# Hybrid decoder block: the last normalisation split into half rows, with low halves begun one product earlier

## The chip, the cores and the metric

The kernel runs on one core of a Trainium2 chip. The metric is device time in microseconds, the median of several runs. A core has five engines with a queue of instructions each, which run side by side and wait for one another by semaphores: PE (TensorE, matrix products into PSUM banks), DVE (VectorE, elementwise), ACT (ScalarE, functions, copies and scalings of rows, with sums along a row on request), POOL (GpSimd, elementwise) and SP (SyncE, which issues DMA transfers). ACT issues some transfers too. An engine works through its queue in the order in which the program wrote it, so an instruction that waits holds up all that stand behind it.

## The reference

One layer on x of 1024 tokens by 1024 columns, in float32: a SwiGLU feed-forward half step, a mixing part with dilated attention and pooling, a second feed-forward half step, and a final row normalisation:

```python
h = h + 0.5 * swiglu(rms_norm(h, ffn1_norm[l]), ffn1_w1[l], ffn1_w3[l], ffn1_w2[l])
...
h = h + merged @ w_out[l]
h = h + 0.5 * swiglu(rms_norm(h, ffn2_norm[l]), ffn2_w1[l], ffn2_w3[l], ffn2_w2[l])
return rms_norm(h, final_norm)
```

with

```python
def rms_norm(x, g):
    y = xf * lax.rsqrt(jnp.mean(xf * xf, axis=-1, keepdims=True) + RMS_EPS)
    return (y * g.astype(jnp.float32)).astype(x.dtype)
```

The change concerns the last two lines: the second product of the second feed-forward step (its output g, 1024 by 2816, times w2, 2816 by 1024), its addition to h, and the final normalisation.

## The kernel before

The 1024 tokens lie in eight tiles of 128 rows, h[0] to h[7], each 128 by 1024. LOWS and HIGHS (line 283) are the slices of the first and the last 512 columns of a tile.

The down product g times w2 is computed as seven products of half-sized blocks instead of eight (the list DOWN, lines 97 to 105). Each product has a left operand (a sum of blocks of g that an earlier stage left in DRAM), a right operand (a block of w2, or the sum or difference of two), and a list of the quarters of the result to which it is added with a sign. A quarter is named (th, n): th = 0 means tiles 0 to 3 and th = 1 tiles 4 to 7, n = 0 the low and n = 1 the high columns. Tiles 0 to 3 are final after the fifth product (index 4, len(DOWN) - 3). The sixth (index 5) is added to the low and the high halves of tiles 4 to 7. The seventh (index 6) is added to the high halves of tiles 4 to 7 alone.

A product is cut into six steps along its inner dimension (PAIRS), five of two 128-deep slices and one of a single slice, so there are 42 steps, 0 to 41; the seventh product is steps 36 to 41. Every operand is held as two parts, high (rounded) and low (the remainder), and a matmul of two operands is three matmuls: high by high, low by high, high by low. A step of two slices is therefore 24 matmuls of 128x128 by 128x512 over the four row tiles, the last step 12.

Class Down writes the order out by hand (nothing is scheduled by a planner):

- `load(i)` (line 645) issues the transfer of step i's left operand on SP, three steps ahead.
- `begin(i)` (line 687) prepares step i, two steps ahead: `sums_w` (line 672) makes the sum of two weight blocks on DVE (tile s, line 684, one 128x512 operation a slice), then `split` (line 652) makes the parts of the right operand (bhi on ACT, line 664; blo, line 668) and of the left one (ahi on ACT, alo). The subtraction that makes a low part runs on DVE, or on POOL in every fourth call of `split`, which is the left operand of every odd step.
- `multiply(i, t)` (line 697) issues step i's matmuls for row tile t into bank t of its product (line 706).
- `add(m, t)` (line 708) adds bank t of product m to the tiles of h, one DVE operation of 128x512 for each quarter (line 711). A product's four adds are issued one a step, in the four steps behind the product's end, ahead of that step's `begin`. For the last product they follow its last two steps, whose matmuls are interleaved by row tile.
- `run` (line 713) is the loop over the steps. Its arguments `after`, called behind each add, and `tick` differ: FFN 1 passes a tick, FFN 2 none.

For FFN 2, `after2` (line 2012) does the final normalisation. For tiles 0 to 3 it is called behind the adds of product 4, for tiles 4 to 7 behind those of product 6. `norm_rows` (line 272) squares a whole row on ACT with its sum (line 259), takes the mean plus epsilon on DVE (line 263), raises it to the power -1/2 on POOL (line 264) and multiplies the row by the result and the gain in one DVE operation of 128x1024 (line 267); then SP stores it. Tile 7 alone is squared and scaled in two halves, low half squared ahead of the other, and its two halves are stored from SP and from ACT.

Buffers: `h_tile` gives one of eight 128x1024 buffers, all held by h[0] to h[7] at that time; the next ones it gives are those of h[0] to h[3] again, once they are read. `row` and `own_row` give other buffers of that size, `small` tiles of a few columns.

Of the kernel before, what the change touches and what calls it, by code (L numbers as in the profile page):

```python
# [10 lines left out]
F32 = mybir.dt.float32  # L11
F32R = mybir.dt.float32r
AF = mybir.ActivationFunctionType
OP = mybir.AluOpType
AX = mybir.AxisListType

P = 128
S = 1024
D = 1024
NT = S // P  # L20
# [3 lines left out]
EPS = 1e-6  # L24
HALF = 512
# [101 lines left out]
def tile_block(  # L127
# [28 lines left out]
    nc = tc.nc  # L156
# [7 lines left out]
    small = ctx.enter_context(sbuf("small", bufs=4))  # L164
# [9 lines left out]
    def row(name):  # L174
        return keep.tile([P, 1024], F32, tag="raw", bufs=RAW_BUFS, name=name)

    def h_tile(name):
        return keep.tile([P, D], F32, tag="h", bufs=NT, name=name)
# [93 lines left out]
    def norm_rows(t, gain, name, alloc=row):  # L272
        y = alloc(f"hn_{name}{t}")
        squares(t, y)
        inverse(t)
        scaled(t, y, gain)
        return y
# [347 lines left out]
    class Down:  # L625
# [26 lines left out]
        def split(self, side, srcs, n):  # L652
            hi, lo = (
                self.dp.tile([P, 2, HALF], F32R, tag=f"{side}{part}", bufs=3, name=f"{side}{part}_{self.name}{n}")
                for part in ("hi", "lo")
            )
            self.n_lo += 1
            whole = len(srcs) == 1 and srcs[0].shape[1] > 1
            eng = gp if self.n_lo % 4 == 0 else ve
            at = 0  # L660
            for src in srcs:
                n = src.shape[1]
                c = slice(at, at + n)
                ac.activation(hi[:, c], src, AF.Copy)  # L664
                for q in range(n if eng is gp else 1):
                    o = slice(q, q + 1) if eng is gp else slice(0, n)
                    d = slice(at + o.start, at + o.stop)
                    eng.tensor_tensor(lo[:, d], src[:, o], hi[:, d].bitcast(F32), op=OP.subtract)  # L668
                at += n
            return hi, lo  # L670
# [42 lines left out]
        def run(self, pool, after, tick=None):  # L713
            def half_tile(tag, n):
                return pool.tile([P, HALF], F32, tag=tag, bufs=4, name=f"{tag}_{self.name}{n}")

            self.half_tile = half_tile
            n = len(self.steps)
            done = []
            for i, (m, s) in enumerate(self.steps):  # L720
                if i < n - 2:
                    for t in range(4):
                        self.multiply(i, t)
                if i == n - 1:

                    for t in range(4):
                        self.multiply(i - 1, t)
                        self.multiply(i, t)
                        self.add(m, t)
                        after(m, t)  # L730
                if done:
                    self.add(*done[0])
                    after(*done.pop(0))
                if s == len(PAIRS) - 1:
                    done = [(m, t) for t in range(4)]
                self.ops.pop(i - 1, None)
                if m == len(DOWN) - 1 and tick is None:
                    raws.depth = max(3, len(PAIRS) + 1 - s)
                if i == 1:
                    next(self.parts, None)  # L740
                if i + 3 < n:
                    self.load(i + 3)
                if i + 2 < n:
                    self.begin(i + 2)
                if i == 0:
                    next(self.parts)
                if tick is not None:
                    tick(i)
# [1260 lines left out]
    def own_row(n):  # L2009
        return pool.tile([P, D], F32, tag="row", bufs=2, name=n)  # L2010

    def after2(m, t):
        if m != len(DOWN) - 3 and m != len(DOWN) - 1:
            return
        if m == len(DOWN) - 1:
            t += 4
        rows = slice(t * P, (t + 1) * P)
        if t < NT - 1:
            nc.sync.dma_start(out[rows, :], norm_rows(t, final_gain, "n4", own_row if t < 4 else row))
            return  # L2020
        y = row("hn_last")
        st = small.tile([P, 4], F32, tag="nlast", name="nst_last")
        for j in range(2):
            c = slice(j * HALF, (j + 1) * HALF)
            ac.activation(y[:, c], h[t][:, c], AF.Square, accum_out=st[:, j:j + 1])
        ve.tensor_scalar(st[:, 0:1], st[:, 0:1], 1.0 / D, EPS, op0=OP.mult, op1=OP.add)
        ve.scalar_tensor_tensor(st[:, 2:3], st[:, 1:2], 1.0 / D, st[:, 0:1], op0=OP.mult, op1=OP.add)
        gp.tensor_tensor(st[:, 3:4], st[:, 2:3], mhalf, op=OP.pow)
        for j in range(2):
            c = slice(j * HALF, (j + 1) * HALF)  # L2030
            ve.scalar_tensor_tensor(y[:, c], h[t][:, c], st[:, 3:4], final_gain[:, c],
                                    op0=OP.mult, op1=OP.mult)
            (nc.sync if j == 0 else nc.scalar).dma_start(out[rows, c], y[:, c])

    with sbuf("steps2", "right") as pool:
        raws.load()
# [94 lines left out]
```

## Time and profile before

| | us |
|---|---|
| runs of before: median of 3 | 1957.8 |
| lowest, highest | 1957.8, 1959.87 |
| profiled execution, first to last instruction | 1955.6 |
| its PE busy | 1914.1 |
| its DVE busy | 1343.5 |
| its ACT busy | 759.4 |
| its POOL busy | 741.1 |

The profile is of one execution, whose own time on the device is the span in the table; the runs are timed around the whole execution, so their median lies a little above. Rows of the timeline read: start and duration in us, engine, line of the kernel, operation, what it writes <- what it reads, shape, and how many like it were merged (x2 for two in a row). In brackets stands how long the engine sat idle before it, and which instruction ended that. An engine's name with a q (ACTq, SPq) is its queue issuing a transfer. Two DVE operations in a row overlap by some 0.08 us, so that a pair of 0.68 us each takes 1.28. Rows of groups read: line, engine, operation, shapes, xcount | busy us, mean ns | idle before it, by what ended it. Rows of windows give busy time and number of instructions of each engine in a stretch, then the granted PE clock, the share of the DMA engines in use and GB/s. Rows of transfers give the queue, how many, KB each, and the median us from issue to landing.

### The profile page before, as it was taken

What the parts mean: (1) busy time and instruction counts of PE and PEld (TensorE: products, weight loads), DVE (VectorE), ACT (ScalarE), POOL (GpSimd) and SP (SyncE); (2) the same over time, 40 slices, a digit from 0 to 9 for tenths busy, and PEclk for the clock granted to TensorE, in tenths of its full rate; (3) what the DMA queues carried; (4) which work ended last, traced back from release to release, by engine and by line L of the source; (5) the groups of instructions that cost most, each with busy time, mean ns of one, the idle gap of its engine ahead of it and who ended that gap; (6) DMA issues with size and microseconds to landing.
All of it is one profiled execution on the core that took longest, in us unless ns stands there. A gap on an engine that the chain in (4) does not pass through costs nothing. (4 is left out here: it accounts for less than half of the span.)

```text
span 1955.6 us, 25018 instructions
## 1 busy us (share of the span) xinstructions
PE 1914.1 (98%) x8938; PEld 1579.7 (81%) x8938; DVE 1343.5 (69%) x2012; ACT 759.4 (39%) x1361; POOL 741.1 (38%) x557
## 2 busy tenths in 40 slices
PE   9999999999999999999998999999999999999997
PEld 7788888888888887888876878887788888878885
DVE  7776556557686876568774886887665556577766
ACT  6333333334344533334344662253333333333343
POOL 5333333332222444445454365543333333322231
PEclk9999999999999999999998999999999999999999
DMA  4155223336465546765658887643523223454653
GB/s 185 44 194 169 85 86 117 121 124 208 156 246 201 167 120 230 232 220 185 232 218 289 241 241 261 253 161 96 190 102 135 82 87 120 139 204 135 212 195 142
DMA packets 147005, 333.57 MB, mean 171 GB/s; under 512 B 20160, under 2 KB 40896, under 8 KB 145344
## 3 DMA queue, kind: packets, MB, share of 16 engines
q1 hardware_dynamic: 138096, 308.00, 45.9%
q10 hardware_dynamic: 8784, 23.96, 3.5%
q8 instruction: 71, 1.16, 0.2%
q14 instruction: 54, 0.44, 0.1%
HBM read 229.61 MB, written 102.30 MB: 170 GB/s over the span
## 5 line engine op out<-in xcount | busy, mean ns | idle before, releaser
L706 PE MATMUL d_f<-bhi_f,alo_f 128*128 128x512 f32 x616 | 240.8, 391 | 2.4 <-POOL alo_f L668 2.2
L706 PE MATMUL d_f<-bhi_f,ahi_f 128*128 128x512 f32 x616 | 240.9, 391 | 0.2 <-ACT ahi_f L664 0.2
L706 PE MATMUL d_f<-blo_f,ahi_f 128*128 128x512 f32 x616 | 240.0, 390 | 0.0
L668 POOL TENSOR_TENSOR alo_f<-g_f,ahi_f 128x512 fp32r<-128x512 f32 x70 | 99.2, 1434 | 298.5 <-ACT ahi_f L664 289.8
L314 PE MATMUL u_mixm<-xhi_t_mix,wc_mixm 128*128 128x512 f32 x608 | 196.0, 393 | 2.7 <-POOL wc_mixm L306 2.3
L314 PE MATMUL u_mixm<-xhi_b_mix,wc_mixm 128*128 128x512 f32 x456 | 149.3, 393 | 2.0 <-DVE y_m L982 2.0
L706 PEld LDWEIGHTS d_f<-bhi_f,alo_f 128*128 128x128 f32 x616 | 115.7, 188 | 29.0 <-POOL alo_f L668 4.0
L314 PEld LDWEIGHTS u_mixm<-xhi_t_mix,wc_mixm 128*128 128x128 f32 x608 | 113.8, 188 | 29.0 <-POOL wc_mixm L306 4.9
L706 PEld LDWEIGHTS d_f<-bhi_f,ahi_f 128*128 128x128 f32 x616 | 115.8, 188 | 24.1 <-ACT ahi_f L664 0.6
L706 PEld LDWEIGHTS d_f<-blo_f,ahi_f 128*128 128x128 f32 x616 | 115.8, 188 | 23.8
L314 PE MATMUL u_mixm<-xlo_t_mix,wc_mixm 128*128 128x512 f32 x304 | 118.6, 390 | 0.0
L306 POOL TENSOR_TENSOR wc_mixm<-s_mixm,wc_mixm 128x512 fp32r<-128x512 f32 x52 | 75.8, 1459 | 99.7 <-ACT wc_mixm L303 84.0
L314 PEld LDWEIGHTS u_mixm<-xhi_b_mix,wc_mixm 128*128 128x128 f32 x456 | 85.7, 188 | 20.7 <-ACT late_hi L1125 2.8
L303 ACT ACTIVATE wc_mixm<-s_mixm 128x512 fp32r<-128x512 f32 x76 | 47.6, 629 | 122.8 <-DVE s_mixm L347 52.1
L314 PE MATMUL u_mixm<-xlo_b_mix,wc_mixm 128*128 128x512 f32 x228 | 88.9, 390 | 0.0
L664 ACT ACTIVATE ahi_f<-g_f 128x1024 fp32r<-128x1024 f32 x84 | 81.8, 974 | 2.0 <-DMA g_f<-gs_f 2.0
L306 POOL TENSOR_TENSOR wc_mixm<-raw,wc_mixm 128x512 fp32r<-128x512 f32 x40 | 60.4, 1515 | 44.9 <-ACT wc_mixm L303 42.0
L664 ACT ACTIVATE bhi_f<-s_f2w 128x512 fp32r<-128x512 f32 x55 | 32.8, 627 | 97.1 <-DVE s_f2w L684 86.8
L1854 PE MATMUL wo<-w_o,o_hi 128*128 128x512 f32 x224 | 69.3, 391 | 0.0
L314 PEld LDWEIGHTS u_mixm<-xlo_t_mix,wc_mixm 128*128 128x128 f32 x304 | 57.2, 188 | 11.7 <-DVE xlo_t_mix L385 0.2
L664 ACT ACTIVATE bhi_f<-s_f1w 128x512 fp32r<-128x512 f32 x55 | 32.9, 630 | 85.1 <-DVE s_f1w L684 80.2
L1616 PE MATMUL yp<-pool_in,wab 128*128 128x512 f32 x192 | 55.7, 426 | 4.2 <-DMA pool_in<-pool 4.2
(1300 smaller groups left out, 5099.8 us busy)
## 6 DMA issues: line engine op xcount, KB each, us to landing
g_f<-gs_f SPq DMA_DIRECT2D x70, 512.0 KB, 4.5
gs_f<-y_f SPq DMA_DIRECT2D x88, 256.0 KB, 2.3
raw<-in_w2a_dram SPq DMA_DIRECT2D x35, 512.0 KB, 4.1
raw<-in_w2b_dram SPq DMA_DIRECT2D x35, 512.0 KB, 4.0
gs_f<-gb_f SPq DMA_DIRECT2D x46, 256.0 KB, 2.3
raw<-in_w1a_dram SPq DMA_DIRECT2D x22, 512.0 KB, 4.6
raw<-in_w3a_dram SPq DMA_DIRECT2D x22, 512.0 KB, 6.3
raw<-in_w1b_dram SPq DMA_DIRECT2D x22, 512.0 KB, 4.5
```

The costliest lines, as they stand in the source:

```text
L303: ac.activation(w[:, 0], src, AF.Copy)
L306: eng.tensor_tensor(w[:, 1], src, w[:, 0].bitcast(F32), op=OP.subtract)
L314: pe.matmul(p, a, b, start=(start and k == 0 and q == 0), stop=(k == 3 and q == 2), skip_group_check=not start)
L664: ac.activation(hi[:, c], src, AF.Copy)
L668: eng.tensor_tensor(lo[:, d], src[:, o], hi[:, d].bitcast(F32), op=OP.subtract)
L706: pe.matmul(self.banks[m][t], l, r, start=(first and q == 0), stop=(last and q == 2))
L1616: pe.matmul(p, a, b, start=(j == 0), stop=(j == 11))
L1854: pe.matmul(banks[m][t], l, r, start=(st == 0 and j == 0 and q == 0), stop=(st == 1 and j == 1 and q == 2))
```

## The change

Three things are edited.

In `split`, a low part that would run on POOL runs on DVE in the last two steps; of those, only the left operand of step 41 is a fourth call. The test holds for both feed-forward steps.

In `run`, where there is no tick (FFN 2), `begin(41)` in step 39 is called ahead of the add of product 5 to tile 7 instead of behind it.

In the final normalisation, tiles 0 to 3 stay as they are. Tiles 4 to 7 are treated alike, in halves. `low_half` is called behind each add of product 5, in steps 36 to 39: it squares the low columns on ACT with their sum, adds epsilon on DVE, and multiplies the low columns by the gain on DVE into a buffer y. The rest follows the adds of product 6: `high_half` squares the high columns, `power` adds the two sums on DVE and raises to -1/2 on POOL, and `send_out` scales the high columns by the row's factor and the gain on DVE, stores them from SP, scales the low columns of y by the row's factor on ACT and stores them from ACT. `send_out` of a tile is called behind the next tile's add and `high_half`, ahead of that tile's `power`. The squares carry the factor 1/1024 inside (a scale of 1/32 ahead of the square).

The order of each engine's queue changes as follows, beside the moved operations. DVE: the add pair of each of tiles 4 to 7 is followed by one 128x1 and one 128x512 operation. ACT: a half square stands ahead of the roundings for step 38, 39 and 40, and a fourth one behind those of step 41; at the end the order is square 4, square 5, scaling and store of 4, square 6, scaling and store of 5, square 7, scaling and store of 6, scaling and store of 7. POOL: without the subtraction of step 41 in each FFN. SP: the same loads in the same order, then four stores of 256 KB instead of three of 512 KB and one of 256 KB. PE: unchanged.

```diff
@@ split @@
             whole = len(srcs) == 1 and srcs[0].shape[1] > 1
-            eng = gp if self.n_lo % 4 == 0 else ve
+            eng = gp if self.n_lo % 4 == 0 and n < len(self.steps) - 2 else ve
             at = 0
@@ run @@
                         self.add(m, t)
                         after(m, t)
+                ahead = i == n - 3 and tick is None
+                if ahead:
+                    self.begin(i + 2)
                 if done:
                     self.add(*done[0])
                     after(*done.pop(0))
...
-                if i + 2 < n:
+                if i + 2 < n and not ahead:
                     self.begin(i + 2)
@@ final normalisation @@
+    ends = {}
+
+    def low_half(t):
+
+        y, st = h_tile(f"n4_{t}"), small.tile([P, 4], F32, tag="nlast", name=f"nst_last{t}")
+        ac.activation(y[:, LOWS], h[t][:, LOWS], AF.Square, scale=D ** -0.5, accum_out=st[:, 0:1])
+        ve.tensor_scalar(st[:, 1:2], st[:, 0:1], EPS, None, op0=OP.add)
+        ve.tensor_tensor(y[:, LOWS], h[t][:, LOWS], final_gain[:, LOWS], op=OP.mult)
+        ends[t] = y, st
+
+    def high_half(t):
+        y, st = ends[t]
+        ac.activation(y[:, HIGHS], h[t][:, HIGHS], AF.Square, scale=D ** -0.5, accum_out=st[:, 2:3])
+
+    def power(t):
+        y, st = ends[t]
+        ve.tensor_tensor(st[:, 2:3], st[:, 2:3], st[:, 1:2], op=OP.add)
+        gp.tensor_tensor(st[:, 3:4], st[:, 2:3], mhalf, op=OP.pow)
+
+    def send_out(t):
+        y, st = ends.pop(t)
+        rows = slice(t * P, (t + 1) * P)
+        ve.scalar_tensor_tensor(y[:, HIGHS], h[t][:, HIGHS], st[:, 3:4], final_gain[:, HIGHS],
+                                op0=OP.mult, op1=OP.mult)
+        nc.sync.dma_start(out[rows, HIGHS], y[:, HIGHS])
+        ac.activation(y[:, LOWS], y[:, LOWS], AF.Copy, scale=st[:, 3:4])
+        nc.scalar.dma_start(out[rows, LOWS], y[:, LOWS])
+
     def after2(m, t):
-        if m != len(DOWN) - 3 and m != len(DOWN) - 1:
-            return
-        if m == len(DOWN) - 1:
-            t += 4
...
+        if m == len(DOWN) - 3:
+            rows = slice(t * P, (t + 1) * P)
+            nc.sync.dma_start(out[rows, :], norm_rows(t, final_gain, "n4", own_row))
+        elif m == len(DOWN) - 2:
+            low_half(4 + t)
+        elif m == len(DOWN) - 1:
+            high_half(4 + t)
+            if t > 0:
+                send_out(3 + t)
+            power(4 + t)
+            if t == 3:
+                send_out(7)
```

More of the change, by code (lines that the diff above doesn't have):

```diff
@@ L2010, in own_row @@
         return pool.tile([P, D], F32, tag="row", bufs=2, name=n)
-    def after2(m, t):
-        if m != len(DOWN) - 3 and m != len(DOWN) - 1:
-            return
-        if m == len(DOWN) - 1:
-            t += 4
[L2017 to L2033, printed above, removed]
```

## The prediction

> **What bounds the kernel now.** The page comes first, for the span and for who is busy; then busy time in windows over the last 25 us, because everything in the diff but one line acts there.
>
> ```profile
> span 1955.6 us, 25018 instructions
> PE 1914.1 (98%) x8938; PEld 1579.7 (81%) x8938; DVE 1343.5 (69%) x2012; ACT 759.4 (39%) x1361; POOL 741.1 (38%) x557
> ```
>
> ```profile
> core 0: us, PE busy (x) PEld busy (x) DVE busy (x) ACT busy (x) POOL busy (x), PEclk, DMA share, GB/s
> ...
> 1925.00:1930.00 5.00, 5.00 (x24) 4.15 (x23) 4.90 (x7) 1.91 (x4) 3.00 (x2) 1.00 0.00 0
> ...
> 1940.00:1945.00 5.00, 3.06 (x14) 2.21 (x12) 3.12 (x5) 1.15 (x2) 0.55 (x1) 1.00 0.26 105
> 1945.00:1950.00 5.00, 0.00 (x0) 0.00 (x0) 2.58 (x5) 2.33 (x6) 0.55 (x1) 0.69 0.34 135
> ```
>
> PE sets the time for nearly the whole span (98%). Two stretches at the end differ. In steps 36 to 41 (1925 to 1930 is typical) DVE is busy 4.90 of 5.00 us beside a full PE: it has no slack to give. After 1943 PE has nothing left, and no engine is busy for much more than half of a window: a chain of waits runs there. The timeline of each engine shows it, DVE first:
>
> ```profile
> 1936.95 0.69 DVE L711 SCALAR_TENSOR_TENSOR h_last<-d_f,h_last 128x512 f32<-128x512 f32 x1 [1.74 <-PE d_f L706]
> 1938.86 0.15 DVE L263 TENSOR_SCALAR nst<-nst 128x1 f32<-128x1 f32 x1 [1.22 <-ACT hn_n L259]
> 1939.68 1.29 DVE L267 SCALAR_TENSOR_TENSOR hn_n<-h_last,nst,gain_final 128x1024 f32<-128x1024 f32 x1 [0.66 <-POOL nst L264]
> 1940.88 0.68 DVE L711 SCALAR_TENSOR_TENSOR h_last<-d_f,h_last 128x512 f32<-128x512 f32 x1
> ...
> 1948.72 0.68 DVE L711 SCALAR_TENSOR_TENSOR h_last<-d_f,h_last 128x512 f32<-128x512 f32 x1
> ...
> 1950.19 0.16 DVE L2027 SCALAR_TENSOR_TENSOR nst_last<-nst_last 128x1 f32<-128x1 f32 x1 [0.73 <-ACT hn_last L2025]
> 1951.01 1.42 DVE L2031 SCALAR_TENSOR_TENSOR hn_last<-h_last,nst_last,gain_final 128x512 f32<-128x512 f32 x2 [0.66 <-POOL nst_last L2028]
> ```
>
> ```profile
> 1937.68 1.06 ACT L259 ACTIVATE hn_n<-h_last 128x1024 f32<-128x1024 f32 x1 [2.67 <-DVE h_last L711]
> ...
> 1949.43 0.63 ACT L2025 ACTIVATE hn_last<-h_last 128x512 f32<-128x512 f32 x1 [2.16 <-DVE h_last L711]
> 1949.97 0.19 ACT L2025 ACTIVATION_READ_ACCUMULATOR hn_last<-h_last 128x1 f32 x1
> 1952.46 0.34 ACTq L2033 DMA_DIRECT2D out_dram<-hn_last  x1
> ```
>
> ```profile
> 1950.43 0.55 POOL L2028 TENSOR_TENSOR nst_last<-nst_last,mhalf 128x1 f32<-128x1 f32 x1 [2.95 <-DVE nst_last L2027]
> ```
>
> ```profile
> 1951.79 0.33 SPq L2033 DMA_DIRECT2D out_dram<-hn_last  x1
> ```
>
> Each tile goes add, square over 1024 columns, mean, power, scaling over 1024 columns, and only then does the next tile's add start: (1948.72 - 1936.95) / 3 = 3.92 us a tile. The last tile takes 3.07 us from add to SP's store and 3.74 to ACT's at 1952.46, which sets the end; 1955.6 - 1952.46 = 3.1 us are landing and close. PE would deliver faster:
>
> ```profile
> 1934.45 0.39 PE L706 MATMUL d_f<-bhi_f,alo_f 128*128 128x512 f32 x1
> 1935.06 0.51 PE L706 MATMUL d_f<-bhi_f,ahi_f 128*128 128x512 f32 x1 [0.22 <-ACT ahi_f L664]
> ...
> 1936.41 0.50 PE L706 MATMUL d_f<-bhi_f,alo_f 128*128 128x512 f32 x1 [0.60 <-POOL alo_f L668]
> 1936.75 0.40 PE L706 MATMUL d_f<-bhi_f,ahi_f 128*128 128x512 f32 x1
> ...
> 1942.67 0.39 PE L706 MATMUL d_f<-bhi_f,alo_f 128*128 128x512 f32 x1
> ```
>
> After the stall on step 41's operands, 26 intervals between 1936.75 and 1942.67 give 0.228 us a matmul, so nine, one tile, 2.05 us. The fourth bank is full at 1943.1 (1942.67 + 0.39), the fourth add starts at 1948.72: 5.6 us of backlog, which is what there is to win.
>
> **The change part by part.** (1) *Step 41's low part goes from POOL to DVE* (one 128x512 subtract, in both FFNs), and in FFN 2 its operands are queued ahead of tile 7's two adds. The rows of these steps:
>
> ```profile
> 1931.86 1.28 DVE L711 SCALAR_TENSOR_TENSOR h_last<-d_f,h_last 128x512 f32<-128x512 f32 x2
> 1933.06 0.68 DVE L684 TENSOR_TENSOR s_f2w<-raw,raw 128x512 f32<-128x512 f32 x1
> 1934.52 0.69 DVE L668 TENSOR_TENSOR blo_f<-s_f2w,bhi_f 128x512 fp32r<-128x512 f32 x1 [0.78 <-ACT bhi_f L664]
> ```
>
> ```profile
> 1914.96 2.99 POOL L668 TENSOR_TENSOR alo_f<-g_f,ahi_f 128x512 fp32r<-128x512 f32 x2 [10.94 <-ACT ahi_f L664]
> 1925.52 3.00 POOL L668 TENSOR_TENSOR alo_f<-g_f,ahi_f 128x512 fp32r<-128x512 f32 x2 [7.57 <-ACT ahi_f L664]
> 1935.09 1.27 POOL L668 TENSOR_TENSOR alo_f<-g_f,ahi_f 128x512 fp32r<-128x512 f32 x1 [6.57 <-ACT ahi_f L664]
> ```
>
> The add pair holds DVE from 1931.86 to 1933.06, so step 41's chain starts 1.20 us earlier without it. On DVE the subtract takes 0.69 instead of 1.27, but follows the previous one's end (1935.21 instead of 1935.09): 0.46 won. Together -1.66. No transfer moves with it: the weights and left operands of step 41 are asked for before, in unchanged order on SP.
>
> In FFN 1 the same subtract costs nothing: DVE has room before it waits for PE there, and if that cover were gone it would cost 0.69. PE itself never waits there, so nothing is won either:
>
> ```profile
> 660.45 0.69 DVE L711 SCALAR_TENSOR_TENSOR h<-d_f,h 128x512 f32<-128x512 f32 x1 [2.13 <-PE d_f L706]
> ```
>
> (2) *Low halves of tiles 4 to 7 in steps 36 to 39.* Each adds a half square on ACT, which has room (1.91 of 5.00), and on DVE a 128x1 operation that waits for it and a 128x512 multiply by the gain. The wait: a square starts 0.71 after its add's start (1948.72 to 1949.43), its sum is there 0.73 later (1950.16), DVE takes it 0.03 after: 1.47, less the 1.20 that the pair of adds fills: 0.27. Then 0.15, then a two-input multiply, not in this trace, priced like the weight sums: 0.60 to the next. One low half: 1.02 us. Everything for the next steps' operands is queued behind that wait on DVE, and ACT's rounding and PE wait for it. Bounds come from the stretch in which POOL splits:
>
> ```profile
> 1915.80 2.70 DVE L684 TENSOR_TENSOR s_f2w<-raw,raw 128x512 f32<-128x512 f32 x2
> ```
>
> Two sums that take 1.28 us alone (0.68 + 0.60) take 2.70 beside POOL's split of 1914.96 to 1917.95: 1.42 lost. Where the new multiply takes the place of a sum in that stretch, DVE loses what it loses already, and the low half costs about 0.42 (wait and 128x1 alone); where it pays the loss anew, 1.02 + 1.42 = 2.44. Tile 5's iteration has no POOL split: 1.02. In those of tiles 4 and 6 there is one (steps 37 and 39), with as many DVE operations fitting under it as before: I take 0.55, near the lower end because the time is lost already. Three of them stand ahead of step 41: 2.1, bounds 1.3 and 7.3.
>
> A rule speaks against this part: the Trainium skill, "SBUF — State Buffer", section "Who interferes with whom", has a DVE instruction with two SBUF inputs and a GpSimd instruction that reads SBUF block each other for a whole instruction; the 2.70 agrees. By the rule taken strictly, each such multiply may pay in full, which is rival B.
>
> PE: net lateness of step 41 is 2.1 - 1.66 = +0.4 (bounds -0.4 and +5.7). Step 39 stalls first: by count back from 1934.45 PE wants its second low part at 1928.8, POOL had it at 1928.52, and two low halves now delay it by 1.6, so PE loses about 1.3 there. Before, it lost 1.4 in step 41 (1934.45 to 1936.41 is 1.96 for three intervals, 0.68, and 0.1 more in restarting); coming there 1.3 later to operands that are 0.4 late, it waits 0.9 less, so the two stalls don't add. The banks come 0.4 late, the fourth at 1943.5.
>
> (3) *The end.* Step 41's split ends on DVE at 1936.36 + 0.4 = 1936.76. Tile 7's adds and low half follow, 1.20 + 1.02, so the first last-product add starts at 1938.9 (before: 1936.95): a loss of 2.0, which the shorter cycle has to earn back. The cycle: add to square 0.71, square and sum 0.73, hand-over 0.03, sum of squares 0.15 = 1.62. The scaling of the tile before, now 0.75 wide (L2031) instead of 1.29, and the power (0.55) lie within the 1.47 of that wait: after the add's 0.6, 0.75 still fits. ACT in a cycle: 0.73, low half scaled 0.63, store issued 0.34 = 1.70, about the same. Three cycles: the fourth add at 1938.9 + 4.9 = 1943.8, just after its bank (1943.5). Then add 0.71, square 0.73, 0.03, sum 0.16, 0.08, power 0.55, 0.03, scaling 0.75, 0.03: 3.07 to SP's store, with ACT's low half beside it. Last store at 1946.9 instead of 1952.46: -5.5.
>
> ```profile
> out_dram<-hn_n SPq DMA_DIRECT2D x5, 512.0 KB, 2.6
> ...
> out_dram<-hn_last ACTq DMA_DIRECT2D x1, 256.0 KB, 2.1
> ```
>
> Two halves now leave at once, which is 512 KB together: between 2.1 and 2.6 to landing; I add 0.3. **Sum: -5.2 us.** The execution would span 1950.4; the runs' median lies 2.2 above the profiled span (1957.8 to 1955.6), so **1952.6 us**.
>
> The low half is scaled on ACT by a per-row scale, which has a neighbour in the trace:
>
> ```profile
> L1087 ACT ACTIVATE pd_hi<-pm,psc 128x512 fp32r<-128x512 f32 x8 | 5.5, 684 | 13.9 <-PE pm L1085 13.9
> L1229 ACT ACTIVATE table<-table 128x512 f32<-128x512 f32 x6 | 3.3, 595 | 6.5 <-PE table L1227 6.5
> ```
>
> The rows give 0.09 more for it, 0.3 over three cycles if ACT sets the pace; that is inside the range. The Trainium skill, "ScalarE: Activation LUTs", section "What ACT_TABLE_LOAD costs", gives about 93 ns for such an operand, and the rows agree.
>
> **The rivals.** *B, the multiply pays beside POOL.* Tiles 4 and 6 at 2.44: step 41 late by 2 x 2.44 + 1.02 - 1.66 = 4.2, fourth add at 1947.6, last store 1950.7, time 1957.8 - 1.8 + 0.3 = 1956.3; with one of the two, 1954.5. For it: 2.70 for 1.28, and DVE busy 4.90 of 5.00. Against: the number of DVE operations under each split stays.
>
> *C, ACT's queue paces the end.* A store issue, which waits on ACT for its own scaling, stands ahead of the next square. At 2.6 a cycle instead of 1.62 the last add comes 2.9 later: 1955.5. For it: ACT's 1.70 already equals the cycle. Against: the issue row has 0.34.
>
> *D, nothing is won*: the four tiles stay serial because a power or a scaling holds DVE as before; about 1957.8. Against: those now wait behind the next add, not ahead of it.
>
> *E, slower.* DVE's new wait ties it to ACT's queue, where the square stands behind the rounding of a left operand, and that can wait for its load. It has once:
>
> ```profile
> 1907.68 1.06 ACT L664 ACTIVATE ahi_f<-g_f 128x1024 fp32r<-128x1024 f32 x1 [1.24 <-DMA g_f<-gs_f]
> ```
>
> A square behind such a wait adds 1.06 + 1.24 to each low half: 3.3. With p per low half the last store is at 1943.8 + 4p (1936.36 - 1.66 + 3p, then 1.2 + p, 4.86, 3.07), so 1957.0 and a time of 1962.7; slower by 0.2% begins at p = 3.06. Against: all four would have to pay it.
>
> **How the numbers follow.** Forecast 0.70, B 0.16, C 0.07, D 0.03, E 0.04. The runs of before spread by 0.1%, so 0.2%, 3.9 us, is what can be told from no change: below 1953.9 is faster. Forecast: 1950.6 (lateness -0.4, no contention at landing, a microsecond of scatter) to 1953.9. B, C and D lie within 0.2%, E is slower: faster 0.70, same 0.26, slower 0.04. The range 1950.6 to 1956.3 takes in B and C.
>
> **What would show it.** Right: adds of the last product about 1.6 to 2.0 us apart; the first at 1938 to 1940, the last 0 to 1 us behind its bank; PE waiting about 1 us for POOL's split in step 39 and less than before in step 41; the scaling multiplies at 0.7 us; eight half stores, the last two together. Wrong: a multiply of 1.8 us in steps 36 or 38 with PE's last matmul after 1945 (B); squares waiting on ACT's own queue in the last four tiles (C); adds still 3.9 us apart (D); DVE idle for a microsecond or more ahead of the 128x1 operations of steps 36 to 39 (E).

## The result, and the profile after

The changed kernel takes 1954.1 us against 1958.12 (medians of 18 runs each). The ratio of the two, taken over all these runs, is 0.9973 with a 95% interval of 0.9966 to 0.998, which is 5.3 us faster (3.9 to 6.7). The medians alone lie 4.0 apart, the means of the same runs 5.1. Forecast were 5.2 us less and a time of 1952.6, in a range of 1950.6 to 1956.3.

The page of the changed kernel begins like this (span, then busy time of each engine):

```profile
span 1954.5 us, 25035 instructions
PE 1917.3 (98%) x8938; PEld 1580.5 (81%) x8938; DVE 1344.2 (69%) x2020; ACT 762.8 (39%) x1371; POOL 738.1 (38%) x555
```

The two profiled executions differ by 1.1 us only (1955.6 and 1954.5). Where the rest went is seen at an instruction that stands ahead of everything that moved in FFN 2: the first weight sum of step 37, which waits for its load. In DVE's timeline, before and then after:

```profile
1911.91 1.29 DVE L684 TENSOR_TENSOR s_f2w<-raw,raw 128x512 f32<-128x512 f32 x2 [1.91 <-DMA raw<-in_w2b_dram]
```

```profile
1915.83 1.30 DVE L684 TENSOR_TENSOR s_f2w<-raw,raw 128x512 f32<-128x512 f32 x2 [2.81 <-DMA raw<-in_w2b_dram]
```

The profiled execution of the changed kernel was 3.92 us late at this point, and 2.66 of that it had already at the last add of product 4 (1898.87 before, 1901.53 after). So below, times are counted from this instruction; call its start the mark. From the mark to the issue of the last store before took 1952.46 - 1911.91 = 40.55 us, after took 35.22: 5.33 less, which agrees with the runs. The last store's row is in ACT's part of the timeline below (1951.05). A second execution of the changed kernel (below) spans 1951.0 and has 35.21 from mark to last store.

DVE after, from the operands of step 41 on:

```profile
1940.02 0.69 DVE L668 TENSOR_TENSOR alo_f<-g_f,ahi_f 128x512 fp32r<-128x512 f32 x1
1940.62 1.28 DVE L711 SCALAR_TENSOR_TENSOR h_last<-d_f,h_last 128x512 f32<-128x512 f32 x2
...
1942.76 0.68 DVE L711 SCALAR_TENSOR_TENSOR h_last<-d_f,h_last 128x512 f32<-128x512 f32 x1
1944.23 0.16 DVE L2031 TENSOR_TENSOR nst_last<-nst_last 128x1 f32<-128x1 f32 x1 [0.79 <-ACT n L2027]
1944.31 0.68 DVE L711 SCALAR_TENSOR_TENSOR h_last<-d_f,h_last 128x512 f32<-128x512 f32 x1
1945.05 0.75 DVE L2037 SCALAR_TENSOR_TENSOR n<-h_last,nst_last,gain_final 128x512 f32<-128x512 f32 x1
...
1945.86 0.68 DVE L711 SCALAR_TENSOR_TENSOR h_last<-d_f,h_last 128x512 f32<-128x512 f32 x1
...
1947.62 0.68 DVE L711 SCALAR_TENSOR_TENSOR h_last<-d_f,h_last 128x512 f32<-128x512 f32 x1
...
1950.12 0.75 DVE L2037 SCALAR_TENSOR_TENSOR n<-h_last,nst_last,gain_final 128x512 f32<-128x512 f32 x1 [0.66 <-POOL nst_last L2032]
```

The four adds of the last product start at 1942.76, 1944.31, 1945.86 and 1947.62: 4.86 us for three cycles, where before took 11.77. The scaling of a tile (1945.05) now runs inside the next tile's wait for its square. ACT in the last tiles:

```profile
1947.42 0.71 ACT L2040 ACTIVATE n<-n,nst_last 128x512 f32<-128x512 f32 x1
1948.15 0.34 ACTq L2041 DMA_DIRECT2D out_dram<-n  x1
1948.54 0.63 ACT L2027 ACTIVATE n<-h_last 128x512 f32<-128x512 f32 x1 [0.42 <-DVE h_last L711]
...
1951.05 0.34 ACTq L2041 DMA_DIRECT2D out_dram<-n  x1
```

Tile 7's add started at 1947.62 and its square at 1948.54, 0.92 later instead of 0.71: ACT was issuing a store until 1948.49. PE's waits after, and its last matmul:

```profile
1920.22 0.50 PE L706 MATMUL d_f<-bhi_f,alo_f 128*128 128x512 f32 x1 [0.55 <-POOL alo_f L668]
1921.93 0.50 PE L706 MATMUL d_f<-bhi_f,alo_f 128*128 128x512 f32 x1 [0.75 <-POOL alo_f L668]
...
1934.05 0.50 PE L706 MATMUL d_f<-bhi_f,alo_f 128*128 128x512 f32 x1 [0.74 <-POOL alo_f L668]
...
1947.02 0.39 PE L706 MATMUL d_f<-bhi_f,alo_f 128*128 128x512 f32 x1
```

The last add (1947.62) now starts 0.2 us behind the end of its last matmul (1947.02 + 0.39); before it was 5.6 behind. The windows of the end show what is left (columns as in the prediction's windows):

```profile
core 0: us, PE busy (x) PEld busy (x) DVE busy (x) ACT busy (x) POOL busy (x), PEclk, DMA share, GB/s
1940.00:1945.00 5.00, 4.93 (x22) 3.83 (x22) 4.01 (x9) 1.45 (x4) 0.53 (x1) 1.00 0.02 3
1945.00:1950.00 5.00, 2.41 (x11) 1.68 (x9) 3.91 (x8) 4.01 (x9) 1.58 (x4) 1.00 0.57 213
```

PE works to 1947.4. In the second of these windows DVE and ACT are each busy for four fifths (3.91 and 4.01 of 5.00), where before had each at about half (2.58 and 2.33).

### The profile page after: what moved, and what is told of

Its sections match the earlier page's. It is cut to its first block, busy times and chain, and to the rows that moved or that the text cites. A ratio compares the mean times of both kernels' runs of the same rounds, so it can differ in the third digit from the quotient of the medians.

```text
span 1954.5 us, 25035 instructions
## 1 busy us (share of the span) xinstructions
PE 1917.3 (98%) x8938; PEld 1580.5 (81%) x8938; DVE 1344.2 (69%) x2020; ACT 762.8 (39%) x1371; POOL 738.1 (38%) x555
## 3 DMA queue, kind: packets, MB, share of 16 engines
q10 hardware_dynamic: 9216, 24.75, 3.6%
```

## The experiments

The theory put to the test: the gain is backlog behind PE, won by the shorter cycle, and the operand edits are needed so that the shorter cycle finds its banks full; the low halves cost step 41's operands about 2.1 us, which the operand edits pay back. Rivals: one of the two parts does all of it (B to D of the prediction have forms of this), the low halves' price lies elsewhere, or ACT's queue sets the cycle. All kernels in one table, counted from the mark (split: end of step 41's last low part; PE: end of the last matmul; adds: the starts of the last product's four). The ratios are to before's runs on the same chip, whose medians lie between 1958.12 and 1959.54. Where a field is empty, the point isn't used. For x2 and x3 the interval takes in 1: how they differ from before is read from their traces, of one execution each.

| | median, us | ratio (95%) | split | PE | adds | last store |
|---|---|---|---|---|---|---|
| before (runs beside after) | 1958.12 | | 24.45 | 31.14 | 25.04, 28.97, 32.89, 36.81 | 40.55 |
| after | 1954.1 | 0.9973 (0.9966 to 0.998) | 24.87 | 31.58 | 26.93, 28.48, 30.03, 31.79 | 35.22 |
| x13, after again | 1952.54 | 0.9962 (0.995 to 0.9975) | 24.87 | 31.57 | 26.93, 28.48, 30.03, 31.79 | 35.21 |
| x1, tail only | 1956.71 | 0.9989 (0.998 to 0.9997) | 27.57 | 35.42 | 28.45, 31.37, 33.42, 35.46 | 38.68 |
| x2, operands only | 1958.16 | 0.9993 (0.9985 to 1.0002) | 22.70 | 29.73 | 23.82, 27.74, 31.66, 35.64 | 39.38 |
| x3, no delay | 1958.45 | 0.9993 (0.9984 to 1.0002) | 24.87 | 31.56 | 26.93, 29.89, 32.86, 35.83 | 38.90 |
| x4, no multiply | 1953.48 | 0.9968 (0.9957 to 0.9979) | 23.09 | 29.80 | 24.55, 26.10, 27.80, 29.84 | 33.07 |
| x5, epsilon late | 1954.31 | 0.9971 (0.9961 to 0.9981) | 24.75 | | | 35.03 |
| x6, low parts on DVE | 1955.8 | 0.9985 (0.9976 to 0.9994) | 25.52 | 32.21 | | 35.87 |
| x8, stores from SP | 1953.41 | 0.997 (0.9959 to 0.9981) | | | 26.92, 28.47, 30.02, 31.60 | 35.10 |
| x9, squares ahead only | 1952.76 | 0.9966 (0.9953 to 0.9978) | 22.70 | 29.72 | 24.70, 26.25, 28.40, 30.54 | 34.21 |
| x11, multiply late | 1950.36 | 0.9955 (0.9942 to 0.9969) | 22.68 | 29.72 | 24.68, 26.23, 28.16, 30.09 | 33.31 |
| x12, x11 with low parts on DVE | 1952.86 | 0.9961 (0.9948 to 0.9973) | 22.67 | 29.36 | 24.67, 26.22, 28.16, 30.09 | 33.31 |
| x14, square's output aside | 1953.84 | 0.9973 (0.9963 to 0.9983) | 24.49 | | 26.21, 27.76, 29.37, 31.27 | 34.56 |

**x1, the tail without the operand edits.** The split of step 41 stays on POOL and behind tile 7's adds.

```diff
-            eng = gp if self.n_lo % 4 == 0 and n < len(self.steps) - 2 else ve
+            eng = gp if self.n_lo % 4 == 0 else ve
...
-                ahead = i == n - 3 and tick is None
+                ahead = False
```

> The halves alone: step 41's low part is back on POOL and its operands are queued behind tile 7's adds, in both FFNs as before. Measure: from the start of step 37's first weight sum on DVE (which a weight load releases) to the issue of the last store; 40.55 us before, 35.22 in the changed kernel. Theory (the queue position is worth its time, because low halves and adds pile up ahead of step 41's split): the split comes 2.2 + 0.5 later than in the changed kernel, the last matmul 2 to 2.7 later, the measure 37.3 to 37.9. Rival (the operand edits are hidden anyway): 35.2.

Measured: 38.68 from mark to last store. It is 1.87 better than before and 3.46 worse than after. All four adds of the last product wait for PE, with 2.03, 1.28, 0.41 and 0.40 us of idle time ahead of them. PE's rows and windows in x1:

```profile
1935.72 0.50 PE L706 MATMUL d_f<-bhi_f,ahi_f 128*128 128x512 f32 x1 [2.08 <-ACT ahi_f L664]
1937.07 0.80 PE L706 MATMUL d_f<-bhi_f,alo_f 128*128 128x512 f32 x1 [0.50 <-POOL alo_f L668]
```

```profile
1936.00:1937.00 1.00, 0.57 (x2) 0.11 (x1) 0.00 (x0) 0.00 (x0) 1.00 (x1) 0.58 0.00 0
1937.00:1938.00 1.00, 0.93 (x2) 0.83 (x3) 0.10 (x1) 0.00 (x0) 0.02 (x1) 0.50 0.00 0
1938.00:1939.00 1.00, 1.00 (x4) 0.71 (x3) 0.59 (x1) 0.37 (x1) 0.00 (x0) 0.50 0.05 16
```

PE waits 2.08 us for step 41's first operand and 0.50 for its low part. The split is 3.1 us later than in before (27.57 against 24.45). Behind the wait the granted clock (the third number from the right) is 0.58, then 0.50 for two microseconds, and the matmuls start 0.43 apart instead of 0.23. Against after, the split is 2.70 later, as expected, but PE's end 3.84: the six intervals from 1937.07 to 1939.70 take 2.63 us, where 0.228 each would make 1.37. These 1.26 us cover the 0.8 by which the run lies above the expected range.

**x2, the operand edits without the tail.** The two other hunks of the diff, put into before.

> The operand edits alone, on the kernel before: step 41's low part on DVE and queued ahead of tile 7's adds; normalisation as before. Same measure (40.55 before, 35.22 changed). Theory: split ready 1.66 earlier, PE's stall in step 41 gone, first add about 1.05 earlier, cycles of 3.9 us unchanged: measure 39.3 to 39.7. Rival (the operand edits bring most of the gain): 37 or less.

Measured: 39.38, inside the range. The split ends 1.75 earlier (22.70; worked out were 1.66), PE does not wait in step 41, and the last bank is full at 29.73 with its add at 35.64: the backlog has grown to 5.9. PE's earlier end is worth 1.2 only because the first add comes earlier. Alone the parts win 1.87 and 1.17, together 5.33: the tail alone runs into PE, the operands alone leave a slow cycle.

**x3, each tile scaled right behind its own power.**

```diff
             high_half(4 + t)
-            if t > 0:
-                send_out(3 + t)
             power(4 + t)
-            if t == 3:
-                send_out(7)
+            send_out(4 + t)
```

> The changed kernel with each tile's scaling and stores right behind its own power, not behind the next tile's add. Theory: DVE holds the next add behind the power and the scaling, the cycle is 0.71 + 0.73 + 0.03 + 0.16 + 0.08 + 0.55 + 0.03 + 0.67 = 2.96 us instead of 1.55 to 1.76, the measure 38.7 to 39.2, the last add 4 us behind its bank. Rival (PE's 2.05 us a tile or ACT sets the pace anyway): 35.2 to 36.

Measured: 38.90, cycle 2.97. In x3's timeline of DVE the power stands on the path again (0.66 idle):

```profile
1940.53 0.68 DVE L711 SCALAR_TENSOR_TENSOR h_last<-d_f,h_last 128x512 f32<-128x512 f32 x1
...
1942.83 0.75 DVE L2037 SCALAR_TENSOR_TENSOR n<-h_last,nst_last,gain_final 128x512 f32<-128x512 f32 x1 [0.66 <-POOL nst_last L2032]
1943.49 0.68 DVE L711 SCALAR_TENSOR_TENSOR h_last<-d_f,h_last 128x512 f32<-128x512 f32 x1
```

Split and PE's end are those of after. Halving the squares (0.44) and the scalings (0.54) brings the cycle from 3.92 to 2.97; scaling one tile behind brings it to 1.62 and is worth 3.7 us of the last store's time.

**x4, the multiply by the gain left out.** The low halves of tiles 4 to 7 are not multiplied by the gain.

```diff
-        ve.tensor_tensor(y[:, LOWS], h[t][:, LOWS], final_gain[:, LOWS], op=OP.mult)
...
-        ac.activation(y[:, LOWS], y[:, LOWS], AF.Copy, scale=st[:, 3:4])
+        ac.activation(y[:, LOWS], h[t][:, LOWS], AF.Copy, scale=st[:, 3:4])
```

> The changed kernel without the multiply of the low halves by the gain (the low half of the output of tiles 4 to 7 then lacks the gain). Theory: three multiplies ahead of step 41's split cost 0.6 each, beside POOL as well, because the number of DVE operations slowed by POOL's split does not change by one for one; split 1.5 to 1.9 earlier, last matmul 1.2 to 1.8 earlier, measure 33.4 to 34.1. Rival (each multiply beside POOL's split pays over 2 us): split 3 or more earlier, PE without a stall in step 41 and the measure at most 33.0.

Measured: 33.07, just between the two ranges for the end, but the split, which is the direct reading, ends 1.78 earlier: 0.59 for each of three multiplies. They cost their own width, also where POOL splits. Tile 4's low half in after, and in x4:

```profile
1918.52 1.28 DVE L711 SCALAR_TENSOR_TENSOR h_last<-d_f,h_last 128x512 f32<-128x512 f32 x2
1919.99 0.15 DVE L2021 TENSOR_SCALAR nst_last<-nst_last 128x1 f32<-128x1 f32 x1 [0.20 <-ACT n L2020]
1920.07 0.68 DVE L2022 TENSOR_TENSOR n<-h_last,gain_final 128x512 f32<-128x512 f32 x1
1920.67 2.36 DVE L684 TENSOR_TENSOR s_f2w<-raw,raw 128x512 f32<-128x512 f32 x2
...
1924.68 1.23 DVE L668 TENSOR_TENSOR alo_f<-g_f,ahi_f 128x1024 fp32r<-128x1024 f32 x1 [0.18 <-ACT ahi_f L664]
```

```profile
1914.03 1.28 DVE L711 SCALAR_TENSOR_TENSOR h_last<-d_f,h_last 128x512 f32<-128x512 f32 x2
1915.51 0.15 DVE L2021 TENSOR_SCALAR nst_last<-nst_last 128x1 f32<-128x1 f32 x1 [0.19 <-ACT n L2020]
1915.58 2.36 DVE L684 TENSOR_TENSOR s_f2w<-raw,raw 128x512 f32<-128x512 f32 x2
...
1919.59 1.23 DVE L668 TENSOR_TENSOR alo_f<-g_f,ahi_f 128x1024 fp32r<-128x1024 f32 x1 [0.26 <-ACT ahi_f L664]
```

From the adds to the left operand's low part is 6.16 in after and 5.56 in x4; before took 5.54 (1914.60 to 1920.14). So where POOL splits, the wait and the 128x1 operation cost 0.02, and the multiply 0.60. For tile 5, with no split on POOL, the same count to the right operand's low part gives 2.66 before, 3.01 in x4 and 3.61 in after: 0.35 for the wait and the small operation, 0.60 for the multiply.

**x5, epsilon added in `power`**, so that DVE's 128x1 operation in the low half goes.

```diff
-        ve.tensor_scalar(st[:, 1:2], st[:, 0:1], EPS, None, op0=OP.add)
...
-        ve.tensor_tensor(st[:, 2:3], st[:, 2:3], st[:, 1:2], op=OP.add)
+        ve.scalar_tensor_tensor(st[:, 2:3], st[:, 2:3], EPS, st[:, 0:1], op0=OP.add, op1=OP.add)
```

> The changed kernel with epsilon added in the last sum (one DVE operation of 128x1 takes both sums and epsilon), so that DVE no longer waits for ACT's half square in steps 36 to 39. Measure: from the start of step 37's first weight sum to the issue of the last store (35.2 in the changed kernel). Theory: three waits of 0.2 and three 128x1 operations of 0.08 to 0.15 go from ahead of step 41's split, which comes 0.7 to 1.1 earlier, and with it PE's end and the measure: 34.1 to 34.6. Rival (the wait is hidden behind POOL's split): 35.0 to 35.2.

Measured: 35.03, a miss for the theory and inside the rival's range. The wait has not gone, it has moved to the multiply (DVE in x5):

```profile
1918.26 0.71 DVE L2021 TENSOR_TENSOR n<-h_last,gain_final 128x512 f32<-128x512 f32 x1 [0.19 <-ACT n L2020]
```

The multiply takes nothing from the square. But the square's elementwise output, of which only the sum is used, is written to the low half of y, and there the multiply writes too.

**x14, the square's unused output moved to the other half of y**, on top of x5.

```diff
-        ac.activation(y[:, LOWS], h[t][:, LOWS], AF.Square, scale=D ** -0.5, accum_out=st[:, 0:1])
+        ac.activation(y[:, HIGHS], h[t][:, LOWS], AF.Square, scale=D ** -0.5, accum_out=st[:, 0:1])
```

> x5 with the square of the low half written to the other half of its buffer. In x5 the multiply waited where the 128x1 operation had waited (0.19), for the square, whose unused output has the multiply's place. Theory: the wait was for the buffer; now it goes, and with the 128x1 operation step 41's split comes 0.5 to 1.0 earlier than in the changed kernel (23.9 to 24.4), the measure is 34.2 to 34.7. Rival (the wait is not on the way to step 41's split, POOL's split and the PE banks are): split at 24.7 as in x5, measure 35.0.

Measured: 34.56, inside the range; the split at 24.49 is 0.1 later than expected. The multiply now follows the adds with no idle time, and beside POOL's split it takes 1.00 instead of 0.68 (DVE in x14):

```profile
1917.03 1.28 DVE L711 SCALAR_TENSOR_TENSOR h_last<-d_f,h_last 128x512 f32<-128x512 f32 x2
1918.22 1.00 DVE L2021 TENSOR_TENSOR n<-h_last,gain_final 128x512 f32<-128x512 f32 x1
1919.15 2.37 DVE L684 TENSOR_TENSOR s_f2w<-raw,raw 128x512 f32<-128x512 f32 x2
```

Counted as above, tile 4's low half gives 6.14 (6.16 in after) and tile 5's 3.27 (3.61). This agrees with x4: the wait costs where POOL is quiet, and nothing where it splits.

**x6, all low parts of the last six steps on DVE**, so that POOL disturbs none of these.

```diff
-            eng = gp if self.n_lo % 4 == 0 and n < len(self.steps) - 2 else ve
+            eng = gp if self.n_lo % 4 == 0 and n < len(self.steps) - 6 else ve
```

> The changed kernel with the low parts of the left operands of steps 37 and 39 on DVE as well, none on POOL in the last product (of both FFNs). Theory: DVE gets 1.15 us more in two iterations, but no operation of it is slowed by POOL any more (1.76 instead of 0.68), so step 41's split comes at about the same time (-0.2 to +0.4), PE's stalls in steps 37 and 39 (1.6 and 0.9 us) go, a stall in step 41 of about the same size takes their place, and the measure stays at 34.9 to 35.6. Rival (PE's stalls in steps 37 and 39 are what makes its end late): measure 33.5 or less.

Measured: 35.87, the split 0.65 later. In x6 the pair of sums takes its own 1.28 again instead of 2.36, but the 128x1024 subtract is now on DVE:

```profile
1918.39 1.23 DVE L668 TENSOR_TENSOR alo_f<-g_f,ahi_f 128x1024 fp32r<-128x1024 f32 x1 [0.18 <-ACT ahi_f L664]
...
1921.67 1.28 DVE L684 TENSOR_TENSOR s_f2w<-raw,raw 128x512 f32<-128x512 f32 x2
```

The subtract with its wait puts the adds behind it 1.40 later, and 1.08 is saved: 0.32 lost in each of two steps. POOL's split is worth having although it slows DVE. The edit acts in FFN 1 too, ahead of the mark, where the measure doesn't see it: there PE waits 1.23 us for a DVE operation (at 639.94), and from the first weight sum of step 37 to the last add it takes 35.02 us (633.93 to 668.95) instead of 33.65 in after (634.16 to 667.81). So 1.4 us of FFN 1 come on top of the 0.65, which agrees with the ratios of x6 and after, 0.9985 and 0.9973: 2.3 us apart.

**x8, the low stores issued on SP**, for rival C.

```diff
-        nc.scalar.dma_start(out[rows, LOWS], y[:, LOWS])
+        nc.sync.dma_start(out[rows, LOWS], y[:, LOWS])
```

> The changed kernel with all eight half stores issued by SP, so that no issue stands in ACT's queue between squares. Theory: ACT's cycle falls from 1.75 to about 1.41, the fourth square starts right behind its add (0.11 instead of 0.24 later), and the last stores are issued one after the other, 0.4 apart: measure 35.0 to 35.3, no change that shows. Rival (ACT's queue paces the end): adds of the last product closer together and the measure 34.6 or less.

Measured: 35.10, as the theory had it. Each square follows its add at once, tile 7's at 0.72 behind it, and the two last stores leave SP one after the other:

```profile
1945.14 0.63 ACT L2027 ACTIVATE n<-h_last 128x512 f32<-128x512 f32 x1 [0.25 <-DVE h_last L711]
```

```profile
1947.49 0.33 SPq L2039 DMA_DIRECT2D out_dram<-n  x1
1947.92 0.40 SPq L2041 DMA_DIRECT2D out_dram<-n  x1
```

ACT's issues cost the last add 0.2 (31.79 to 31.60) and the last issue 0.1. The span ends 38.28 after the mark (1951.1 - 1912.82) instead of 38.67, because the two last stores leave 0.43 apart instead of 0.15 (see Landing below); the runs, at 0.997 and 0.9973, do not tell x8 and after apart.

**x9, only the squares ahead.** For tiles 4 to 6 ACT still squares the low half early, but DVE does nothing for it then; it scales both halves by factor and gain behind the next add. Epsilon as in x5.

```diff
+        if t == 7:
+            ve.tensor_tensor(y[:, LOWS], h[t][:, LOWS], final_gain[:, LOWS], op=OP.mult)
...
+        if t == 7:
+            ac.activation(y[:, LOWS], y[:, LOWS], AF.Copy, scale=st[:, 3:4])
+        else:
+            ve.scalar_tensor_tensor(y[:, LOWS], h[t][:, LOWS], st[:, 3:4], final_gain[:, LOWS],
+                                    op0=OP.mult, op1=OP.mult)
```

> A version meant to be faster: in steps 36 to 38 only ACT's half squares are ahead; DVE gets neither the 128x1 operation nor the multiply there, and scales both halves of tiles 4 to 6 behind the next add (two operations of 0.75); tile 7's low half keeps its multiply and its scaling on ACT; epsilon in the last sum. Theory: step 41's split comes 2.2 earlier than in the changed kernel (about 22.7 after the measure's start), PE has no stall in step 41 and ends 1.8 earlier; DVE's cycle is 1.9, below PE's 2.05, so the fourth add follows its bank: measure 33.0 to 33.4, 2 us less than the changed kernel. Rival (DVE's longer scaling holds the adds): measure 34 to 35.

Measured: 34.21. Split (22.70) and PE's end (29.72) are as expected, as early as in x2. The cycle is not: 2.15 instead of 1.9. DVE's four operations alone take 2.00 of it (0.60, 0.67, 0.66 and 0.07), so the 1.9 was summed too low, and 0.14 more is a wait: both scalings need the power's result, and neither can fill the time until it is there (DVE in x9):

```profile
1942.45 0.68 DVE L711 SCALAR_TENSOR_TENSOR h_last<-d_f,h_last 128x512 f32<-128x512 f32 x1
1943.19 0.75 DVE L2037 SCALAR_TENSOR_TENSOR n<-h_last,nst_last,gain_final 128x512 f32<-128x512 f32 x1
1943.86 0.75 DVE L2043 SCALAR_TENSOR_TENSOR n<-h_last,nst_last,gain_final 128x512 f32<-128x512 f32 x1
```

**x11, the multiply late.** As x9, but the low half of tiles 4 to 6 is multiplied by the gain right behind the last product's add, which needs no power, and scaled on ACT as in the changed kernel.

```diff
     def high_half(t):
         y, st = ends[t]
         ac.activation(y[:, HIGHS], h[t][:, HIGHS], AF.Square, scale=D ** -0.5, accum_out=st[:, 2:3])
+        if t < 7:
+            ve.tensor_tensor(y[:, LOWS], h[t][:, LOWS], final_gain[:, LOWS], op=OP.mult)
```

> A version meant to be faster: as x9 (in steps 36 to 38 nothing but ACT's half squares), but the low halves of tiles 4 to 6 are multiplied by the gain on DVE right behind the tile's last add, where DVE waits for ACT anyway, and scaled on ACT as in the changed kernel. Measure: from the start of step 37's first weight sum to the issue of the last store (35.2 changed, 34.2 in x9). Theory: split of step 41 at 22.7 after the start as in x9, PE's end at 29.7; DVE's cycle is 0.60 + 0.60 + 0.67 + 0.08 = 1.95, below PE's 2.05, so the fourth add is at most 0.4 behind its bank: measure 33.0 to 33.5. Rival (the scaling waits for the power and the cycle stays at x9's 2.15): 34.0 or more.

Measured: 33.31, cycle 1.93. The multiply fills the time of ACT's square (DVE in x11):

```profile
1937.62 0.68 DVE L711 SCALAR_TENSOR_TENSOR h_last<-d_f,h_last 128x512 f32<-128x512 f32 x1
1938.22 0.68 DVE L2029 TENSOR_TENSOR n<-h_last,gain_final 128x512 f32<-128x512 f32 x1
1938.82 0.75 DVE L2039 SCALAR_TENSOR_TENSOR n<-h_last,nst_last,gain_final 128x512 f32<-128x512 f32 x1
...
1939.55 0.68 DVE L711 SCALAR_TENSOR_TENSOR h_last<-d_f,h_last 128x512 f32<-128x512 f32 x1
```

With x12 it is the shortest, by this measure, of the versions that leave no work out: 1.9 us less than after from mark to last store. By the runs its median is 1950.36 beside 1952.54 for the changed kernel on the same chip; the intervals of their ratios overlap (0.9942 to 0.9969 and 0.995 to 0.9975), so that it beats before is measured, and that it beats after rests on the profile.

**x12, x11 with the low parts of steps 37 and 39 on DVE** (x6's line added).

> x11 with the low parts of steps 37 and 39 on DVE too. Theory: with no multiply there, two weight sums beside POOL's split lose 1.42 (2.70 for 1.28), more than the 1.15 + 0.2 that the low part costs on DVE, so step 41's split comes no later (22.3 to 22.8) and PE's stall in step 37 (0.45) goes: PE's end 29.2 to 29.4, measure 32.6 to 33.2. Rival (as in x6, DVE loses more by it than it wins): split at 23.3 or later, measure 33.5 or more.

Measured: 33.31 again, 0.1 above the range. PE ends 0.36 earlier, and nothing follows from it: the adds start where they did, behind DVE's own queue. In x11 PE does not set the end any more. As in x6, the edit costs 1.4 us in FFN 1, ahead of the mark: from the first weight sum of step 37 there to the last add x12 takes 35.07 us (633.60 to 668.67) and x11 33.60 (633.63 to 667.23). So x12 is the longer of the two as a whole, and its median lies 2.5 us above x11's, though with five runs each the intervals overlap.

**x13, the changed kernel a second time.**

> The changed kernel itself, beside x11, x12 and x14 on one chip. If the measure from step 37's first weight sum to the last store is a property of the program, it is 35.1 to 35.3 again (and step 41's split at 24.9, PE's end at 31.6), whatever the profiled span comes to; if it drifts with the execution like the span does (the span was 1955.6 before and 1954.5 changed, while the medians lie 4 us apart), it differs by a microsecond or more.

Every point of the table agrees to 0.01 with the first execution, while the span differs by 3.5 us. The mark separates what the program does from what an execution brings along.

## Why the prediction was right

*Step 41's operands.* The edits were put at -1.66, x2 has -1.75: the subtract on DVE starts 0.61 behind the one ahead of it (1931.00 and 1931.61 in x2), not at its end, as the sum had it. The low halves were put at 2.1 together (0.55, 1.02, 0.55); measured are 0.62, 0.95 and 0.60, which makes 2.17 (in tile 5 the 128x1 operation holds DVE for 0.08 instead of 0.15). Net +0.4 was forecast, +0.42 is measured (24.45 to 24.87).

*The reason for 0.55 was wrong, though the number held.* The prediction let the multiply be free beside POOL's split and charged the wait. x4 shows the reverse: the multiply costs 0.60 everywhere, and the wait and the small operation cost 0.02 there, because the pair of sums behind them, starting later, loses 1.08 beside POOL instead of 1.42 (2.36 for 2.70). The two errors cancelled. The wait itself was put down to the small operation; x5 and x14 show that the shared buffer alone would hold DVE as long.

*PE.* In step 39 a loss of 1.3 was forecast; the wait there is 0.74, with restarting about 1.0. The waits in step 37 (0.55 and 0.75) were not in the working. Neither matters for the end, as argued: PE's end follows step 41's operands, 6.71 behind the split in after and 6.69 in before. The banks came 0.44 later where 0.4 was worked out.

*The tail.* The first add was put 2.0 later and came 1.89 later; three cycles were put at 4.86 and took 4.86. The intervals are 1.55, 1.55 and 1.76, so the 1.62 of the sum was 0.07 too much for the first two: the sum of squares holds the next add for 0.08 (1944.23 to 1944.31), not for 0.15. In the third cycle ACT's queue came in, which was put at 1.70. That the total is exact is chance. x3 confirms that the power and the scaling were off the path only through the delay.

*The last chain* was put at 3.07 to SP's scaling and store and took 3.28: the 0.21 is tile 7's square behind ACT's store issue, and x8 takes it away. The sum had ACT's last store beside SP's; it left 0.15 behind it (1951.05 and 1950.90). These two, less the 0.14 by which the first add came earlier than put (1.89 later instead of 2.03), turn the -5.55 of the sum into -5.33.

*Landing.* From the last issue to the end of the span is 3.45 (1954.5 - 1951.05), before 3.14: +0.3, as forecast for two halves that leave at once. The other runs bear it out: 3.15 with 0.67 us between the two last issues (x2), 3.18 with 0.43 (x8), 3.45 with 0.15 (after), 3.75 with 0.03 (x3).

*FFN 1.* Step 41's subtract was put at nothing there. From the first weight sum of step 37 in FFN 1 to the last add before takes 33.53 us (633.56 to 667.09) and after 33.65 (33.61 in x13): some 0.1 more.

*The rivals.* B: the slowed multiply did not come; it takes 0.68 in all of steps 36 to 39, that of tile 4 (1920.07) too, while POOL splits from 1918.88 to 1921.88. The loss falls on the pair of sums behind it, 1.08 in all. C: ACT's queue costs 0.2 in the third cycle, not 1 in each. D: the cycle fell from 3.92 to 1.62. E: the wait of DVE is 0.19 or 0.20 in each of the four low halves; no square stood behind a late load in the profiled executions. That it cannot happen is not shown.

## What to carry to other kernels

Where the last engine's work lies microseconds behind the one that feeds it, count the backlog first: it bounds what a shorter cycle can win, and what makes the feeder late must be moved in the same change, or the parts win what they win alone, here 3.0 of 5.3. Ahead of the end put only the work of an engine that has room (here the squares on ACT), and fill another engine's wait with work that needs none of its results (x11). Measure from an instruction ahead of the change when executions drift by as much as the change is worth, and look separately at every place ahead of it where the same edit acts (x6 and x12 in FFN 1).

## What the runs showed of the hardware that was not expected

*The granted clock.* In x1 it fell to 0.50 behind 2.08 us of idle PE. In x5 it fell as well, behind two waits of 0.68 and 0.71 us in step 37:

```profile
1921.00:1923.00 2.00, 2.00 (x6) 1.53 (x5) 1.65 (x4) 1.87 (x3) 0.00 (x0) 0.50 0.31 111
```

The changed kernel had two waits of 0.55 and 0.75 in the same place and kept a clock of 1.00. The Trainium skill, "TensorE: Matmul & The Clock Gate", section "What's actually happening", has the clock fall after an idle window of some 3.4 us, counted in windows that run on their own. Half speed agrees with the 0.50. A whole idle window is what ends full speed in before: PE's last matmul ends at 1943.06, and the clock falls at 1946.92. In x1 and x5 the measurement differs: no idle stretch of 3.4 us lies ahead of the fall.

The windows themselves show in the traces: half speed lasts from 1936.16 to 1939.58 in x1 and from 1920.31 to 1923.72 in x5, 3.41 us each, and within one execution the changes of the granted clock lie whole multiples of 3.413 us apart (in x5 also 1131.83), at a place that differs between executions. But the window ahead of the fall was not idle throughout: PE was busy for 1.33 of its 3.41 us in x1 (1932.75 to 1936.16) and for 2.02 in x5 (1916.89 to 1920.30). The changed kernel's two waits lie in one window as well (1918.55 to 1921.96), with PE busy for 2.11, and the clock stayed. So the place of the window does not set x5 and the changed kernel apart, and where the limit lies is not shown: elsewhere a window with 1.68 busy kept the clock (x8, 1367.05 to 1370.46) and one with 2.08 lost it (x14, 1059.37 to 1062.78).

*DVE beside POOL.* POOL's split of two operations (3.00 us) cost the pair of sums 1.42 in before. In after and in x4 it cost 1.08, 0.34 less, where DVE had first waited 0.20 and done a 128x1 operation, 0.35 in all. In x14, with the multiply in that place, the loss is 0.32 on the multiply and 1.09 on the pair, 1.41 again. So a short wait of DVE beside POOL's split was free in each case, and work put in its place was slowed. The sums suggest that the wait is time which POOL would have taken anyway; no run took the two engines apart.
